# One background side for the adaLN blocks, unforced norm chains and one side for both attentions' heads in a two-layer hybrid DiT kernel

## The chip, the cores and the metric

The kernel runs on one core of a Trainium2 chip. The metric is the device time of one execution in microseconds: the median of the runs shown, and the profiled execution where the trace is read. TensorE (PE) multiplies, VectorE (DVE), ScalarE (ACT) and GpSimd (POOL) do the elementwise work, and SyncE (SP) issues nearly all of the transfers.

## The reference, cut to what matters

Two layers work on 256 latent tokens `x` and 256 context tokens `h`, each of 1024 channels, all in float32. In the last layer the context leaves after the mixer's inputs, so that what follows runs on 256 tokens instead of 512.

```python
for l in range(DEPTH):                                   # DEPTH = 2
    sh1, sc1, g1, sh2, sc2, g2, sh3, sc3, g3 = split(silu(c) @ w_mod[l] + b_mod[l], 9)   # and the same of c_ctx
    x = x + 0.5 * g1 * swiglu(modulate(rms_norm(x, norm_g[l, 0]), sh1, sc1), ...)        # and h
    y, yc = token_mixer(modulate(rms_norm(x, norm_g[l, 1]), sh2, sc2), ...)              # GLA, neighbourhood attention, GQA
    x = x + g2 * y                                       # h only if l < DEPTH - 1
    x = x + 0.5 * g3 * swiglu(modulate(rms_norm(x, norm_g[l, 2]), sh3, sc3), ...)
```

`token_mixer` projects `u` by `w_in`, runs the three branches (four GLA heads, 16 neighbourhood heads, eight GQA heads on two key heads), and merges them as a sum of `sigmoid(gate_i) * (y_i @ w_branch[i])`, times `w_out`. `w_mod[l]` is 1024 x 9216: 18 blocks of 512 columns a layer.

## The kernel before

**Weights.** Every large product is a chain of `chunk` items: a tile of 512 KB of weights (`w_raw`) is loaded through SP's queue, ScalarE rounds it to `w_hi`, GpSimd computes the rest `w_lo`, and TensorE multiplies three times (hi x hi, hi x lo, lo x hi). `RAW_BUFS` raw tiles and `SPLIT_BUFS` = 3 split pairs are in flight; a tile is loaded when the splitter has done with the one `RAW_BUFS` before it. The products are `up` and `dn` in the FFNs, `pf` (channels on partitions) and `pt` (tokens on partitions) elsewhere.

**Sides.** The order of instructions is fixed when the program is built. `Clock` keeps an estimated time for each engine, from `took`; its PE time is "now". Work beside the main chain is written as generators whose operations (`Gated`) yield until the clock says that their inputs are ready; VectorE, ScalarE and GpSimd operations of a side also yield while their engine's estimate is more than `QUEUE` = 1 us ahead. `tick`, called after every six products, resumes each of them once (`round`): first the `urgent` list, then the named `sides`. `finish(name)` gives a side the hurry and resumes it until it is over; where nothing can go on, the clock's PE time jumps (`round_or_stall`), and the engine stands idle on the chip. `flush` does this for the urgent list, and every `call` item begins with a `flush`.

**adaLN blocks.** `first_load` and `first_u` compute four blocks at the start. A block in `mod_gen` loads eight `mod_w` tiles (256 KB each) and sums them, scaled by `silu(c)` and `silu(c_ctx)`, into `mod_acc`: 16 VectorE operations on 128x512. After two blocks, TensorE reduces over partitions (`mod`), ScalarE copies, and TensorE transposes (`mod_t`). The steps are paced, `MOD_SPAN / len(extra)` us a block: twelve blocks in layer 0's first FFN, four in its last, ten in layer 1's first. `prog.finish(("ffn", l, i))` stands before the second half's `down`. Six blocks are held back as fillers: `mod_prefetch` loads their weights, and `norm_fill` multiplies them on TensorE inside a norm.

**Norms.** At the end of an FFN or of the mixer, `norm_start` puts two chains (`norm_chain`, tokens 0 to 255 and 256 to 511) on the urgent list: sums of squares on TensorE into `n_ss`, `rsqrt` on VectorE (`rs_v`, `rs_s`, `rs_y`, `rs_a`), a diagonal `n_diag`, its broadcast by TensorE, then `n_t`, `u_hi` and `u_lo` for each of eight channel tiles. The first chain stops after four tiles until the second has four. The next product calls `need(r, k)` for each tile.

**Mixer.** GLA heads run as side `gla` (two lanes) beside `gla_project` and `nat_project(l, 0)`; then side `nat` (eight pairs of heads, two lanes), and, after `finish("nat")` and `split_y1` in `ready1`, side `gqa` (eight heads, two lanes), which `ready2` finishes. In layer 0 `ready1` stands in branch 1 after two gates; in layer 1 it is `middle` of branch 0.

Of the kernel before, what the change touches and what calls it, by code (L numbers as in the profile page):

```python
# [18 lines left out]
P = 128  # L19
# [18 lines left out]

RAW_BUFS = 4
SPLIT_BUFS = 3  # L40
# [5 lines left out]
QUEUE = 1.0  # L46
MOD_SPAN = 270.0

# [5 lines left out]
class Clock:  # L54
# [59 lines left out]
    def took(self, engine, name, ins, outs):  # L114
        n = max([x.free_size() for x in ins + outs] + [1])
        if engine == "PE":
            return 0.11 if name == "transpose" else self.matmul(ins, outs[0])
        if engine == "ACT":
            return 0.18 + n / 1200 + (0.2 if len(outs) > 1 else 0.0)
        if engine == "POOL":  # L120
            return 0.1 + n * 0.00235
        both = sum(not x.space == bass.MemoryType.PSUM and x.free_size() > 64 for x in ins) > 1
        return 0.1 + n / 960 * (1.5 if both else 1.1)

# [76 lines left out]
class Program:  # L201
# [4 lines left out]
    def __init__(self, nc, rpool, wpool):  # L206
        self.nc = nc
        self.rpool = rpool
        self.wpool = wpool
        self.clock = Clock()  # L210
        self.items = []
        self.sides = {}
        self.urgent = []
        self.free = [0.0] * 4
        self.force = False
        self.first = False
        self.hurry = None
        self.wakes = []
        self.paced = {}
        self.kept = set()  # L220
        self.chains = {}
# [105 lines left out]
    def round(self):  # L327
        self.wakes = []
        n = self.clock.count
        self.first = True  # L330
        for g in list(self.urgent):
            if not self._resume(g):
                self.urgent.remove(g)
        self.first = False
        for name in list(self.sides):
            if name in self.sides:
                self._step(name)
        return self.clock.count > n

    def round_or_stall(self):  # L340
        sides, urgent = len(self.sides), len(self.urgent)
        if self.round() or len(self.sides) < sides or len(self.urgent) < urgent:
            return
        wakes = [w for w in self.wakes if w is not None]
        assert wakes, "the sides wait for each other"
        self.clock.t["PE"] = max(self.clock.now + 0.01, min(wakes))
# [83 lines left out]
def tile_backbone(ctx: ExitStack, tc: tile.TileContext, I: dict, out: bass.AP):  # L430
# [114 lines left out]

    st = {}

    def first_load():
# [15 lines left out]
        for j in range(4):  # L564

            ws = []
            for kt in range(KT):
                w = S("mod_w")
                src = I["w_mod"][0, kt * P : (kt + 1) * P, : 2 * D].rearrange("p (s n) -> p s n", s=2)
                sync.dma_start(w.rearrange("p (s n) -> p s n", s=2), src[:, :, j * 256 : (j + 1) * 256])  # L570
                ws.append(w)
            st["first_w"].append(ws)
            prog.load(2 * (j + 1) if j < 2 else 4)

# [121 lines left out]

    def mod_load(l, g):
        ws = []
        for kt in range(KT):
            w = S("mod_w")  # L700
            sync.dma_start(w, I["w_mod"][l, kt * P : (kt + 1) * P, g * 512 : (g + 1) * 512])
            ws.append(w)
        return ws

    def mod_gen(blocks, key, us):

        acc = []
        for l, g in blocks:
            yield from prog.pace(key, 0.0)
            ws = mod_load(l, g)  # L710
            acc += [S("mod_acc") for _ in range(2)]
            for kt in range(KT):
                yield from prog.pace(key, us / KT)
                for r in range(2):
                    c = scv[:, kt, r : r + 1]
                    a = acc[r - 2]
                    if kt == 0:
                        yield from gdve.tensor_scalar(a, ws[kt], c, None, op0=ALU.mult)
                    else:
                        yield from gdve.scalar_tensor_tensor(a, ws[kt], c, a, op0=ALU.mult, op1=ALU.add)  # L720
# [11 lines left out]
        for j, (l, g) in enumerate(blocks):  # L732
            bias = st["vec", l][:, 4 * g : 4 * g + 4].unsqueeze(2).broadcast_to([P, 4, 2])
            yield from gdve.tensor_tensor(st["mod", l][:, 4 * g : 4 * g + 4, :], src[:, :, j, :, 0], bias, op=ALU.add)
        prog.release(1)

    def mod_side(name, blocks, us):
        prog.side(name, lambda: (mod_gen(blocks[i : i + 2], name, us) for i in range(0, len(blocks), 2)))

# [71 lines left out]
    def norm_start(l, i, r, n):  # L811
        prog.later(norm_chain(l, i, r, n))

# [61 lines left out]

    def ffn(l, i, which, n, square, extra=(), ahead=(), lead=None):

# [126 lines left out]

        if extra and not lead:
            mod_side(("ffn", l, i), extra, MOD_SPAN / len(extra))
        for a, b in ((0, 12), (12, NH)):
            for mp in range(a // 2, b // 2):
# [5 lines left out]
                if both and lead:  # L1014
                    prog.call(lambda: load_vectors(1))
                    mod_side(("ffn", l, i), extra, MOD_SPAN / len(extra))
            if a == 0:
                prog.call(gates)
                if late_vectors:
                    prog.call(late_vectors.pop())  # L1020
            for fp in range(4):
                if a and fp == 0:
                    if extra:
                        prog.finish(("ffn", l, i))
                    mod_prefetch(("ahead", l, i), ahead)
# [599 lines left out]

    def nat_project(l, g, nq):

# [4 lines left out]

        for kind, c0, tiles in (("q", C_NQ, nq // P), ("k", C_NK, TT), ("v", C_NV, TT)):
            raw = []

# [142 lines left out]

    def gqa_head(h, need_ctx):
        kv = h // 4  # L1780
        res = [{}]
        yield from prog.until(lambda: ("qrot", h // 4) in st and ("qk", kv) in st)
        yield from turn_split("qq", h, st["qrot", h // 4], h % 4, None, False)
# [22 lines left out]

    def branch(l, i, n, ready=None, middle=None):

        th = {}

        def gate(mp):
            def ev(m, ps):
                t = S("m_t")[:, :n]
                act.activation(t, ps, AF.Tanh, scale=0.5)
                th[2 * mp + m] = t

            proj_f(l, C_GATE + D * i + 256 * mp, n, ev)

        def product(mp):
            def ev(m, ps):  # L1820
                f = 2 * mp + m
                t = th.pop(f)
                if i == 0:
# [20 lines left out]

        gate(0)
        gate(1)
        if ready:
            ready()
        product(0)
        product(1)  # L1850
        if middle:
            middle()
        for mp in (2, 3):
            gate(mp)
            product(mp)

    def merge_out(l, n):
# [13 lines left out]
        def last_fn(kh):  # L1871
# [18 lines left out]
            return fn  # L1890

        prog.call(gates)
        for mp in range(4):
            if mp == 3 and n > LAT:
# [16 lines left out]
    def mixer(l, ahead):  # L1911
# [4 lines left out]
        def reset():  # L1916
            st["y2"] = [None] * KT
            st["zs"] = {}
            st["gq"], st["gk"], st["gv"] = {}, {}, {}
            for key in [k for k in st if k == "fg" or k[0] in ("gw2", "nraw", "nv", "qrot", "qk", "qv")]:  # L1920
                del st[key]
# [5 lines left out]
        gla_project(l, 1, nq)  # L1927
        nat_project(l, 0, nq)
        prog.finish("gla")
        prog.finish(("nat", "q", 0))  # L1930
        prog.finish(("nat", "k", 0))
        prog.side("nat", lambda: (nat_pair(l, j, need_ctx) for j in range(8)), lanes=LANES)
        nat_project(l, 1, nq)

        def ready1():
            prog.finish("nat")
            prog.call(lambda: split_y1(n))
            for kind, first in (("k", 0), ("q", 0), ("q", 4)):
                prog.finish(("gqa", kind, first))
            prog.side("gqa", lambda: (gqa_head(h, need_ctx) for h in range(8)), lanes=LANES)  # L1940

        if need_ctx:
            gla_gate(l, nq)
            branch(l, 0, n)
            gqa_project(l, nq)
            branch(l, 1, n, ready=ready1)
        else:
            gqa_project(l, nq)
            gla_gate(l, nq)
            branch(l, 0, n, middle=ready1)  # L1950
            branch(l, 1, n)

        def ready2():
            prog.finish("gqa")

# [22 lines left out]
    prog.call(first_tokens)  # L1978
    blocks = iter([(l, g) for l in range(DEPTH) for g in range(18)])

    def take(n):
        return [next(blocks) for _ in range(n)]

    take(4)
    late_vectors = [lambda: turn_vectors(1)]
    for l in range(DEPTH):
        last = l == DEPTH - 1
        n = LAT if last else NT
        extra = take((12, 10)[l])
        ahead = take(1)  # L1990
        ffn(l, 0, 0, NT, (l, 1), extra, ahead, None if l else lead)
        norm(l, 1, NT, ahead)
        ahead = take(2 if last else 1)
        mixer(l, ahead)
        norm(l, 2, n, ahead)
        if last:
            ffn(l, 2, 1, n, None)
        else:
            extra = take(4)
            ahead = take(1)  # L2000
            ffn(l, 2, 1, n, (l + 1, 0), extra, ahead)
            norm(l + 1, 0, n, ahead)
    prog.run()
# [41 lines left out]
```

## Time and profile before

| | |
|---|---|
| median of three runs | 2944.79 us (2941.56 to 2947.43) |
| profiled execution | 2946.19 us |
| its span, first to last instruction | 2944.1 us |
| TensorE busy | 2773.4 us (94%), 15547 products |
| VectorE, GpSimd, ScalarE busy | 1644.7, 1287.3, 1008.3 us |
| mean granted clock of TensorE | 0.973 |
| bytes read from HBM | 342.83 MB |

The profiled execution takes 2.1 us more than its span. Busy TensorE is not TensorE at its peak: a product's record is longer than the distance to the next one, and at a granted clock of 0.5 it runs at 1.2 GHz instead of 2.4.

### The profile page before, as it was taken

Reading aid. Unit: us, or ns where it says so; the run is one execution under the profiler, and the core shown is the slowest. Engines: PE = TensorE matmul, PEld = TensorE weight load, DVE = VectorE, ACT = ScalarE, POOL = GpSimd, SP = SyncE. Lnnn points to the kernel's source line nnn. Section 1 sums busy time; section 2 is a strip of 40 time slices with the busy share of each in tenths; the row PEclk is TensorE's granted clock in tenths of the full one; section 3 lists DMA queues with packets and bytes.
Section 4 is the critical chain, followed back from the end, with each engine's and each line's share of the span. In section 5 each row is a group of like instructions: output and inputs, shape, how many; then the busy total and the mean of one; then the engine's idle time right before and its main releaser. Section 6 shows DMA issues by size and latency. Waiting matters only on the chain.

```text
span 2944.1 us, 39725 instructions
## 1 busy us (share of the span) xinstructions
PE 2773.4 (94%) x15547; PEld 2320.4 (79%) x15547; DVE 1644.7 (56%) x2969; ACT 1008.3 (34%) x1599; POOL 1287.3 (44%) x585
## 2 busy tenths in 40 slices
PE   8999768999999999998999979998899998899999
PEld 6888647777777788887878878886787777799899
DVE  5666646545785285446344266756455669764422
ACT  2222212343443244322223212222244345454443
POOL 3444313233333442333444434443333445548787
PEclk9999979999999999999999989999899999999999
DMA  7544532122222331333334325444322323336554
GB/s 240 173 151 151 185 108 73 53 65 81 75 71 71 89 89 58 97 97 108 126 118 129 115 87 169 167 155 148 100 72 79 91 78 114 93 113 208 177 182 151
DMA packets 295647, 346.46 MB, mean 118 GB/s; under 512 B 15541, under 2 KB 238806, under 8 KB 295460
## 3 DMA queue, kind: packets, MB, share of 16 engines
q1 hardware_dynamic: 294964, 343.58, 37.2%
q8 instruction: 122, 2.00, 0.3%
q14 instruction: 65, 0.53, 0.1%
q0 software_dynamic: 320, 0.28, 0.0%
q10 hardware_dynamic: 176, 0.07, 0.0%
HBM read 342.83 MB, written 1.05 MB: 117 GB/s over the span
## 4 chain that ended last, share of the span: by engine, by line
PE 85%; DVE 9%; issue 4%; POOL 1%; ACT 1%; DMA 0%; SPq 0%; DVEq 0%; POOLq 0%; ACTq 0%
PE up L169 27%; PE pf L169 19%; PE dn L169 14%; PE pt L169 14%; PE a_s L196 2%; DVE mod_acc L196 2%; PE a_t L196 2%; PE n_o L196 1%; PE g_o L196 1%; PE q_o L196 1%; DVE a_p L196 1%; POOL w_lo L196 1%; DVE rs_a L196 1%; PE g_U L196 1%; PE a_qk L196 1%
## 5 line engine op out<-in xcount | busy, mean ns | idle before, releaser
L196 POOL TENSOR_TENSOR w_lo<-w_raw,w_hi 128x1024 fp32r<-128x1024 f32 (+1 forms) x508 | 1227.5, 2421 | 1586.1 <-ACT w_hi L196 1496.4
L196 ACT CAST w_hi<-w_raw 128x1024 fp32r<-128x1024 f32 (+1 forms) x504 | 521.0, 1037 | 973.0 <-issue 327.6
L169 PE MATMUL up<-u_hi,w_lo 128*128 128x512 f32 (+1 forms) x1504 | 530.0, 352 | 10.1 <-POOL w_lo L196 10.1
L169 PE MATMUL up<-u_hi,w_hi 128*128 128x512 f32 (+1 forms) x1504 | 532.5, 354 | 2.7 <-DVE u_hi L169 2.5
L169 PE MATMUL up<-u_lo,w_hi 128*128 128x512 f32 (+1 forms) x1504 | 529.6, 352 | 0.9 <-DVE u_lo L196 0.7
L169 PE MATMUL dn<-ff_h,w_hi 128*128 128x512 f32 (+1 forms) x1528 | 400.4, 351 | 0.0
L196 DVE SCALAR_TENSOR_TENSOR mod_acc<-mod_w,scv,mod_acc 128x512 f32<-128x512 f32 x364 | 372.5, 1087 | 2.0 <-DMA mod_w<-w_mod 1.8
L169 PEld LDWEIGHTS up<-u_hi,w_hi 128*128 128x128 f32 x1504 | 286.6, 191 | 54.9 <-issue 15.3
L169 PEld LDWEIGHTS up<-u_hi,w_lo 128*128 128x128 f32 x1504 | 286.6, 191 | 48.9 <-POOL w_lo L196 11.2
L169 PEld LDWEIGHTS up<-u_lo,w_hi 128*128 128x128 f32 x1504 | 286.8, 191 | 38.2 <-DVE u_lo L196 0.9
L169 PEld LDWEIGHTS dn<-ff_h,w_hi 128*128 128x128 f32 x1528 | 269.7, 191 | 39.5 <-issue 1.7
L169 PE MATMUL dn<-ff_h,w_lo 128*128 128x512 f32 (+1 forms) x764 | 267.2, 350 | 0.0
L169 PE MATMUL pt<-w_hi,u_hi 128*128 128x512 f32 x640 | 261.5, 409 | 0.3 <-ACT g_q L169 0.3
L169 PE MATMUL pf<-u_hi,w_hi 128*128 128x256 f32 (+1 forms) x736 | 248.3, 337 | 4.1 <-DVE fg L169 1.8
L169 PE MATMUL pt<-w_hi,u_lo 128*128 128x512 f32 x640 | 250.1, 391 | 0.0
L169 PE MATMUL pt<-w_lo,u_hi 128*128 128x512 f32 x640 | 249.9, 391 | 0.0
L169 PE MATMUL pf<-u_hi,w_lo 128*128 128x256 f32 (+1 forms) x736 | 238.6, 324 | 5.6 <-POOL w_lo L196 5.6
L169 PE MATMUL pf<-u_lo,w_hi 128*128 128x256 f32 (+1 forms) x736 | 238.0, 323 | 0.0
L169 DVE TENSOR_TENSOR ff_h<-ff_a,up 128x512 f32<-128x512 f32 (+1 forms) x88 | 53.5, 621 | 323.2 <-PE up L169 287.6
L169 PE MATMUL pf<-y,w_hi 128*128 128x512 f32 (+1 forms) x768 | 194.3, 343 | 1.4 <-ACT y L196 1.2
L169 DVE SCALAR_TENSOR_TENSOR x<-dn,ff_g,x 128x256 f32<-128x256 f32 x112 | 47.1, 478 | 215.2 <-PE dn L169 215.2
L169 PEld LDWEIGHTS pf<-u_hi,w_hi 128*128 128x128 f32 x736 | 142.5, 194 | 23.7 <-issue 10.2
(226 smaller groups left out, 4017.1 us busy)
## 6 DMA issues: line engine op xcount, KB each, us to landing
w_raw<-ffn_w_in SPq DMA_DIRECT2D x176, 512.0 KB
w_raw<-w_in SPq DMA_DIRECT2D x168, 512.0 KB
mod_w<-w_mod SPq DMA_DIRECT2D x288, 256.0 KB
w_raw<-ffn_w_out SPq DMA_DIRECT2D x80, 512.0 KB
w_raw<-w_branch SPq DMA_DIRECT2D x48, 512.0 KB
w_raw<-w_out SPq DMA_DIRECT2D x16, 512.0 KB
w_raw<-ffn_w_out SPq DMA_DIRECT2D x16, 256.0 KB
n_rel<-nat_rpb SPq DMA_DIRECT2D x32, 109.5 KB
```

Of the source, the lines that this page charges most:

```text
L169: return real(*args, **kw)
L196: return real(*args, **kw)
```

## The change

`RAW_BUFS` goes from 4 to 3. VectorE's estimate in `took` goes up. `norm_start` appends to a list of its own, `norms`, which `round` resumes first and which `flush` does not drain. One side `mods` takes 26 blocks in order through the whole program, 42 us a block, resumed last in every round; it loads `mod_w` tiles three steps ahead instead of eight at once; it starts no new pair while `paused` (from `finish("gla")` to `ready2`). `mod_need` gives it the hurry where a norm, a gate or a residual needs its columns. The six fillers stay the same blocks. In the mixer the second group's neighbourhood `q` is projected before `finish("gla")`; the eight pairs and the eight GQA heads are one side, `heads`, with two lanes; `ready1` waits for all `y1` only. In layer 0 the GQA heads wait for the split `y1`; in layer 1 they don't, branch 0 has no stop, and branch 1 begins with all gates of branches 1 and 2.

```diff
-RAW_BUFS = 4
+RAW_BUFS = 3
...
-MOD_SPAN = 270.0
+MOD_PACE = 42.0
...
-        return 0.1 + n / 960 * (1.5 if both else 1.1)
+        return 0.15 + n / 960 * (1.8 if both else 1.15)
...
     def round(self):
...
-        for g in list(self.urgent):
-            if not self._resume(g):
-                self.urgent.remove(g)
+        for waiting in (self.norms, self.urgent):
+            for g in list(waiting):
+                if not self._resume(g):
+                    waiting.remove(g)
         self.first = False
-        for name in list(self.sides):
+        for name in sorted(self.sides, key=lambda name: name == "mods"):
...
-            prog.load(2 * (j + 1) if j < 2 else 4)
+            prog.load(min(2 * (j + 1), RAW_BUFS))
...
     def mod_gen(blocks, key, us):
         acc = []
+        yield from prog.until(lambda: key not in prog.paused or prog.hurry == key)
         for l, g in blocks:
             yield from prog.pace(key, 0.0)
-            ws = mod_load(l, g)
+            yield from prog.until(lambda: ("vec", l) in st)
+            ws = []
             acc += [S("mod_acc") for _ in range(2)]
             for kt in range(KT):
                 yield from prog.pace(key, us / KT)
+                while len(ws) < min(KT, kt + 3):
+                    k = len(ws)
+                    w = S("mod_w")
+                    sync.dma_start(w, I["w_mod"][l, k * P : (k + 1) * P, g * 512 : (g + 1) * 512])
+                    ws.append(w)
...
+    def mod_need(l, k0, k1):
+        def run():
+            prog.hurry = "mods"
+            while any((l, g) in st["mod_blocks"] and (l, g) not in st["mod_done"] for g in range(k0 // 4, k1 // 4)):
+                prog.round_or_stall()
+            prog.hurry = None
+        prog.call(run)
...
     def norm_start(l, i, r, n):
-        prog.later(norm_chain(l, i, r, n))
+        prog.norms.append(norm_chain(l, i, r, n))
...
             if a == 0:
+                mod_need(l, 24 * i + 16, 24 * i + 24)
                 prog.call(gates)
...
                 if a and fp == 0:
-                    if extra:
-                        prog.finish(("ffn", l, i))
+                    if square:
+                        mod_need(square[0], 24 * square[1], 24 * square[1] + 16)
...
-        gate(0)
-        gate(1)
+        done = st["gated"]
+        for b in gates or (i,):
+            for mp in range(4 if gates else 2):
+                if (l, b, mp) not in done:
+                    gate(mp, b)
+                    done.add((l, b, mp))
         if ready:
             ready()
...
         nat_project(l, 0, nq)
+        nat_project(l, 1, nq, "q")
         prog.finish("gla")
-        prog.finish(("nat", "q", 0))
-        prog.finish(("nat", "k", 0))
-        prog.side("nat", lambda: (nat_pair(l, j, need_ctx) for j in range(8)), lanes=LANES)
-        nat_project(l, 1, nq)
+        prog.call(lambda: prog.paused.add("mods"))
+        heads = [lambda j=j: nat_pair(l, j, need_ctx) for j in range(8)]
+        heads += [lambda h=h: gqa_head(h, need_ctx, (lambda: "y1" in st) if need_ctx else None) for h in range(8)]
+        prog.side("heads", lambda: (make() for make in heads), lanes=LANES)
+        nat_project(l, 1, nq, "kv")
...
         else:
             gqa_project(l, nq)
             gla_gate(l, nq)
-            branch(l, 0, n, middle=ready1)
-            branch(l, 1, n)
+            branch(l, 0, n)
+        branch(l, 1, n, ready=ready1, gates=None if need_ctx else (1, 2))

         def ready2():
-            prog.finish("gqa")
+            prog.finish("heads")
+            prog.call(lambda: prog.paused.discard("mods"))
```

## Rows read from the trace of the kernel before

**Rows 1.** The profile's page, part 1: busy time and its share, by engine.

```profile
PE 2773.4 (94%) x15547; PEld 2320.4 (79%) x15547; DVE 1644.7 (56%) x2969; ACT 1008.3 (34%) x1599; POOL 1287.3 (44%) x585
```

**Rows 2.** Waits of TensorE, whole span: total us, times, longest.

```profile
PE mod L196 <- DVE mod_acc L196: 55.8, 8, 20.6
PE n_ss L196 <- DVE n_diag L196: 37.4, 5, 8.8
...
PE up L169 <- POOL w_lo L196: 10.1, 4, 5.7
```

**Rows 3.** Timeline, layer 0's first FFN: start, us, instruction, idle before.

```profile
338.53 4.02 SPq L169 DMA_DIRECT2D mod_w<-w_mod  x8
...
338.64 1.07 PE L196 MATMUL mod<-mod_acc,ones 128*32 128x512 f32 x8 [1.25 <-DVE mod_acc L196]
...
342.18 0.88 DVE L196 TENSOR_SCALAR mod_acc<-mod_w,scv 128x512 f32<-128x512 f32 x2 [0.17 <-DMA mod_w<-w_mod]
...
373.74 1.94 PE L196 MATMUL mod<-mod_acc,ones 128*32 128x512 f32 x8 [19.74 <-DVE mod_acc L196]
...
398.10 1.94 PE L196 MATMUL mod<-mod_acc,ones 128*32 128x512 f32 x8 [20.55 <-DVE mod_acc L196]
...
401.49 1.20 PE L169 MATMUL dn<-ff_h,w_hi 128*128 128x512 f32 x2
```

**Rows 4.** Timeline of TensorE at the same place of layer 1.

```profile
2057.41 1.94 PE L196 MATMUL mod<-mod_acc,ones 128*32 128x512 f32 x8 [9.58 <-DVE mod_acc L196]
...
2060.82 1.20 PE L169 MATMUL dn<-ff_h,w_hi 128*128 128x512 f32 x2
```

**Rows 5.** Tile `mod_acc` up to 420: ns min/median/max, first and last start.

```profile
L196 DVE SCALAR_TENSOR_TENSOR mod_acc<-mod_w,scv,mod_acc x168: 735/741/2911, 73.1 to 397.2; 128x512 f32<-128x512 f32 x168
...
L196 PE MATMUL mod<-mod_acc,ones x48: 592/617/1062, 134.9 to 399.0; 128*32 128x512 f32 x48
```

**Rows 6.** Chain that ended last, two pieces: start, us, products.

```profile
239.16 21.55 PE up L169 x95
...
401.84 18.23 PE dn L169 x72
```

**Rows 7.** Timeline, norm before layer 0's mixer.

```profile
469.20 0.15 DVE L196 TENSOR_SCALAR rs_v<-n_ss 128x2 f32<-128x2 f32 x1
...
472.68 1.22 PE L196 MATMUL n_ss<-n_diag,ones 128*128 128x256 f32 x2 [8.77 <-DVE n_diag L196]
...
473.83 3.64 PE L169 MATMUL mod<-mod_w,scv 128*32 128x512 f32 x16
```

**Rows 8.** Windows: busy PE, PEld, DVE, ACT, POOL; clock; DMA share; GB/s.

```profile
455.00:478.00 23.00, 12.59 (x81) 8.65 (x81) 18.77 (x59) 3.07 (x5) 5.72 (x4) 0.70 0.20 55
...
540.00:600.00 60.00, 56.28 (x412) 45.22 (x411) 38.50 (x91) 22.12 (x37) 12.66 (x6) 1.00 0.16 45
...
2440.00:2540.00 100.00, 86.56 (x581) 74.40 (x580) 93.69 (x197) 48.43 (x88) 59.12 (x27) 0.91 0.39 115
2540.00:2560.00 20.00, 14.02 (x94) 10.62 (x94) 10.73 (x31) 8.62 (x19) 8.15 (x7) 0.83 0.31 89
...
2760.00:2940.00 180.00, 179.64 (x1495) 179.04 (x1494) 48.53 (x59) 77.62 (x106) 146.83 (x63) 1.00 0.55 172
```

**Rows 9.** Tiles `g_oT`, `n_raw`, `q_o` in layer 0: first and last start.

```profile
L196 PE MATMUL g_oT<-ident,g_o x32: 270/272/330, 585.5 to 691.7; 128*128 128x128 f32 x32
...
L169 DVE COPY n_raw<-pt x2: 692/692/692, 701.6 to 704.3; 128x512 f32<-128x512 f32 x2
...
L196 PE MATMUL q_o<-a_pt,q_v x72: 277/283/285, 1168.1 to 1207.7; 128*128 128x256 f32 x72
```

**Rows 10.** Costliest groups of the page: busy, mean ns, idle before.

```profile
L196 POOL TENSOR_TENSOR w_lo<-w_raw,w_hi 128x1024 fp32r<-128x1024 f32 (+1 forms) x508 | 1227.5, 2421 | 1586.1 <-ACT w_hi L196 1496.4
L196 ACT CAST w_hi<-w_raw 128x1024 fp32r<-128x1024 f32 (+1 forms) x504 | 521.0, 1037 | 973.0 <-issue 327.6
...
L196 DVE SCALAR_TENSOR_TENSOR mod_acc<-mod_w,scv,mod_acc 128x512 f32<-128x512 f32 x364 | 372.5, 1087 | 2.0 <-DMA mod_w<-w_mod 1.8
```

## What the change should do, worked out before it ran

> **What bounds the kernel now.** I read the page first: TensorE is busy 94% of the span, so only its holes can be won [rows 1]. I then took the table of waits for TensorE, because it says which engine ends each hole [rows 2]: VectorE's modulation sums (`mod_acc`) 55.8 us, the norm's `n_diag` 37.4 us in five waits, POOL's `w_lo` 10.1 us. The timeline and the windows put places to them.
>
> The largest hole is in the first FFN. At its second `down`, `prog.finish` asks for all twelve modulation blocks, and two of the six pairs aren't summed yet: TensorE sits idle 19.74 us, does the pair's small products, sits 20.55 us more, and its first `dn` product starts at 401.49 [rows 3]. With the idle time that began at 373.74 - 19.74 = 354.0 that is 47.5 us. The same happens in layer 1's first FFN: 9.58 us, back at work at 2060.82, so 13.0 us from 2047.83 [rows 4]. Why pairs come late is seen in the sums: they begin at 73.1, the first pair's products stand at 134.9, the fourth's at 338.64 [rows 3, 5], so a pair takes (338.64 - 134.9)/3 = 67.9 us, where `MOD_SPAN` asks for 45. A product of 512 columns takes 21.55/95 = 0.227 us [rows 6], the sides are looked at every six of them, 1.36 us, and a step due after 2.81 us is taken at the third look, 4.08; sixteen are 65.3.
>
> Four norms each have a hole: after the second half's sums of squares TensorE waits 8.77 us for `n_diag`, then comes the block held for filling (473.83 to 477.47), and only then the first `pf` product [rows 7]. `flush` writes the whole chain out before anything else. In layer 1's attention TensorE is busy 86.56 of 100 us and then 14.02 of 20, at clocks 0.91 and 0.83, while VectorE is busy 93.69 of 100 [rows 8].
>
> **The change, part by part.** The sum is made against the profiled execution, 2946.2 us (span 2944.1 and 2.1 around it), which is 1.4 over the median of the runs.
>
> Side over the whole program, 42 us a block: a step is due after 5.25 us and taken at the fourth look, 5.44; a pair is 16 x 5.44 = 87 and the 2.6 that it took beyond its steps before. The first pair's last step is the fifteenth after its start, so the pairs stand near 73 + 82 = 155, 245 and 334. The gates of the first half want blocks 4 and 5 (about 170), the second `down` wants 6 to 9, three pairs, at 354: in time by some 20 us. The hole of 47.5 us then goes. Its two pairs' products stay (1.07 us for `mod` at the full clock [rows 3], about half of that for `mod_t`, 3.0 in all); the 72 `dn` products behind the hole took 18.23 instead of 16.3 us [rows 6], which comes back too: **-46.5 us**. Layer 1's sums now start in layer 0, pause for the attentions and go on when its GQA heads end, at 1207.7 before [rows 9] and some 60 us sooner now; the six pairs that are left take 6 x 89.6 = 538 us and stand near 1690, long before the second `down` at 2047. The 13.0 us less 1.5 for the pair's products, and some 1.5 of slow clock back as behind the first hole: **-13 us**. The fillers are the same six blocks as before, and cost the same.
>
> Where this work goes: 26 blocks of some 16 x 1.09 = 17 us of VectorE [rows 10], of which some four pairs pass into layer 0's norms, its GLA part and its third FFN. VectorE was busy 38.50 of 60 us in the GLA part [rows 8]; eleven steps of two sums, 11 x 2 x 1.087 = 24 us, fill it to 62.5. The sums come last in every round, so they slide rather than the heads, but the heads slow too. The cover: GLA's last product stood at 691.7, the projection that hides it ended at 704.3 [rows 9], 13 us later, and the moved `q` projection adds 4 x 24 x 0.227 = 22 us before `finish("gla")`. Of the 35 us I let the heads use up nearly all and charge **+5** (bounds 0 and 24, the sums' whole share of that stretch). These sums' median is 741 ns and their longest 2911 [rows 5], next to POOL's `w_lo` of 2421 on average [rows 10]: a sum can stand a whole `w_lo` long. The Trainium skill ("SBUF — State Buffer", "Who interferes with whom") calls this an exclusive lock between VectorE with two inputs in SBUF and GpSimd, the second one blocked to the end. By it every sum put into the GLA part could hold a head's operation for 2.4 us; by the rows' mean of 1.087 it is 0.35 over the median. I go by the mean.
>
> Norm chains not forced: the fill (3.64 us) and the first half's four `k` steps (4 x 12 x 0.120 = 5.8 us, 0.120 from 180 us over 1495 products [rows 8]) can now run in the hole: 9.4 us for 8.77. But the second half's `rs_v` starts at 469.20 only; its broadcast ends at 472.68 + 1.22 = 473.9, and three short VectorE steps on, near 476, stands its first `u` [rows 7]: TensorE waits again for some 3 us. That leaves some 6 a norm where no sums run beside it (the last of the four). In the other three, four steps of sums (8 to 9 us of VectorE) fall into the chain, and I leave them 3. 6 + 3 x 3.3 = **-16 us**, bounds 0 and 4 x 8.77 = -35. Behind the norm the mixer's short loads on SP, POOL's memsets for the decay weights and ScalarE's table load now pass the rest of the chain; the chain waits for none of them, so I put nothing on them.
>
> Shared side and gates first: layer 0's attentions have no hole to win, and their order hardly changes (GQA heads still wait for `y1`). In layer 1 the stop in the middle of branch 0 goes, and two gates (four loads of weights) more stand before `finish("heads")`. To be won are 13.4 + 6.0 us of idle time, and the clock, 100 x 0.09 + 20 x 0.17 = 12 us at most, part of it in idle time [rows 8]: 28 together. VectorE at 94% is not relieved, so I take less than half: **-12 us**, bounds 0 and -28.
>
> VectorE's new price (0.15 + 1.8 n/960: 1.11 us for a sum of 512) fits the mean of 1.087 [rows 10]; the old one was 0.9. The other five waits for `mod_acc`, 55.8 - 49.9 = 5.9 us [rows 2 to 4], should mostly go: -4. Loading `mod_w` three at a time instead of eight (eight took 4.02 us of the queue of SP [rows 3]) lets `w_raw` pass: `w_lo`'s 10.1 us shrink by -4 [rows 2]. **-8 us**, bounds 0 and -12.
>
> Three raw buffers instead of four: tightest where a load of weights is used up in 24 x 0.120 = 2.9 us, in the last FFN. A buffer's round is a cast (1.04), a `w_lo` (2.42) [rows 10] and the transfer. The first of eight loads issued at 338.53 was there at 342.18 [rows 3], 3.65 us, behind a large one. 1.04 + 2.42 + 3.65 = 7.1 is under 3 x 2.9 = 8.6: **0**; if the round were 1 us over, its 60 loads would cost 0.33 each, 20 us. At the start, the fourth load isn't needed before a buffer of the split is free.
>
> Sum: -46.5 - 13 + 5 - 16 - 12 - 8 = -90.5. 2946.2 - 90.5 = 2855.7, and 1.4 off for the median: **2854 us**.
>
> **The rivals.**
> - Only the two stops go (A). The norm's hole moves behind its first four steps and layer 1 stays bound by VectorE, which speaks for it at 94% busy; TensorE's idle time while VectorE is free in the norms speaks against. -46.5 - 13 - 8 + 5 = -62.5: 2882.
> - All holes go (B): -46.5 - 13 - 35 - 28 - 8 = -130.5: 2814. The clock would have to stay full.
> - The pairs aren't in time (C), so that the side does not do what it says at 354: one pair is awaited at full speed, as the second of the old hole was (401.49 - 377 = 24 us). 2854 + 24 = 2878. A look more per step, 6.8 us, would do it; a margin of one pair's quarter speaks for it, the rate of before, which the count of looks explains to 4%, against.
> - Slower than before (D): dearer VectorE prices make the planner hold the heads back, and in layer 1 they end with nothing but four products of branch 1 (23 us) to hide them. Its heads took some 310 us, from about 2330 to 2640 (the last hole of [rows 8] ends at 2560, eight GQA heads later comes `ready2`). A 512-column sum's price rises by 1.11/0.9 = 1.23, a two-column step's from 0.10 to 0.15, 1.5. If the heads stretched by 1.3, they would be 93 us late at `finish("heads")`: 2854 + 12 + 93 = 2959. It decides from (2945 - 2866)/310 = 1.25 on. Against it: the prices only come near what the operations take, and those of one input rise by about 1.1.
> - A gap left in a norm costs more than itself (E). Around a norm the granted clock is 0.70 over 23 us, and it was 0.83 in 20 us of layer 1 with holes in them [rows 8]; what was lost there is 20 x 0.17 = 3.4 us. If each norm's 3 us gap cost 3.4 more, 2854 + 4 x 3.4 = 2868. The Trainium skill ("TensorE: Matmul & The Clock Gate", Part 1) has an idle TensorE fall to 1.2 GHz and come back only after sustained work, and the `dn` products after the long hole [rows 6] agree.
>
> **How the numbers follow.** Forecast 0.52, A 0.20, B 0.12, C 0.07, D 0.04, E 0.05. The likeliest by itself spans 2836 to 2872 (norms and layer 1 each half wrong). For 8 in 10 I go up to past A and C, with most of GLA's 24 on top of the lower one (2882 + 14), and down to B: 2814 to 2896. Measured runs differ by 0.2%, about 6 us, which is what can't be told from no change. Faster 0.94 (all cases but D, and 0.02 of A and C, where the GLA part would add its worst), same 0.02, slower 0.04.
>
> **What would show it.** Right: no wait for `mod_acc` over 3 us near 350 and 1950; TensorE's waits for `n_diag` well under 37 us, with `pf` or `up` products between a norm's sums of squares and its second broadcast; sums of `mod_acc` all through the GLA part and the third FFN; VectorE near 55 of 60 us there; last FFN as long as before. Wrong: a wait before `a_qk` or at the last `g_oT` of layer 0; idle time after the last gate of layer 1 while `a_t` and `q_o` finish; `w_hi` waiting for `w_raw`.

## The result, and the profile after

The changed kernel takes 2882.24 us (median of four runs, 2878.06 to 2883.48), against 2946.11 for the kernel before beside it: a ratio of 0.9783 [0.9766, 0.98], so 63.9 us less. The forecast was 2854, with 2814 to 2896 as the range. Two thirds of the forecast gain came; the missing third has one place, which the parts of the span show. They are cut at the same product of each kernel's trace (a norm runs from the start of the last main product ahead of it to the end of the next 192 main products, 96 in the last):

```
us of the profiled execution           before   after   forecast change   measured
layer 0, first FFN                      434.0   378.4        -50.5          -55.6
layer 1, first FFN                      361.5   346.5        -13            -15.0
the five norms                          205.3   213.3        -20             +8.0
layer 0, mixer and its output           817.2   819.2         +5             +2.0
layer 1, mixer and its output           568.9   560.6        -12             -8.3
start, other FFNs                       551.9   553.0          0             +1.1
```

(The forecast's -8 for prices and loads is split here as it was made: -4 for the sums' other waits to the first FFN, -4 for `w_lo` to the norms.) Every line but one is within 6 us. The norms were to give 20 and took 8. The profiled execution is the fastest of the four, so its parts add up to 67.8 us and not to 63.9.

TensorE's waits over the whole span say what stands there now (total us, times, longest). They are to be read against [rows 2]:

```profile
PE up L169 <- POOL w_lo L196: 16.0, 4, 6.8
PE pf L169 <- POOL w_lo L196: 8.7, 3, 4.8
...
PE pf L169 <- DVE u_hi L196: 7.0, 3, 4.6
PE pf L169 <- DVE u_lo L196: 5.7, 6, 2.4
...
PE n_ss L196 <- DVE n_diag L196: 5.1, 3, 4.2
PE up L169 <- DVE u_lo L196: 4.8, 5, 2.4
...
PE up L169 <- DVE u_hi L196: 4.1, 5, 1.2
...
PE mod L196 <- DVE mod_acc L196: 2.7, 2, 2.1
```

`mod_acc` has gone from 55.8 us to 2.7 and `n_diag` from 37.4 to 5.1, as the prediction asked. But `w_lo` has gone from 15.7 us to 24.7, and the `u` tiles of the norms from 0.9 to 21.6, so these two took up 29.7 of the 32.3 us that `n_diag` gave. (The 15.7 are the 10.1 in `up` of [rows 2] and, in the kernel before, these in `pf`.)

```profile
PE pf L169 <- POOL w_lo L196: 5.6, 4, 2.0
```

The side itself is in time. This is the tile `mod_acc` (first and last start), and then the first `dn` of the second half in TensorE's timeline, 53.6 us sooner than in [rows 3] and with no idle time before it:

```profile
L196 PE MATMUL mod<-mod_acc,ones x104: 592/605/617, 145.6 to 1814.5; 128*32 128x512 f32 x104
```

```profile
347.69 0.39 PE L169 MATMUL up<-u_hi,w_lo 128*128 128x512 f32 x1
347.92 0.61 PE L169 MATMUL dn<-ff_h,w_hi 128*128 128x512 f32 x2
```

The first three pairs' products stand at 145.6, 234.5 and 323.2, where 155, 245 and 334 were forecast. The last pair stands at 1814.5 and not near 1690, and is still 190 us ahead of the second `down` of layer 1 (2004.71).

These windows answer to [rows 8] (us; busy time of PE, of PEld, which loads its weights, of DVE, ACT and POOL; granted clock, DMA share, GB/s). Four lie in the GLA part, one in layer 0's last FFN, two in layer 1's attention, and the last in layer 1's last FFN.

```profile
480.00:540.00 60.00, 56.90 (x425) 49.03 (x425) 44.77 (x89) 23.00 (x39) 14.74 (x6) 0.97 0.27 84
540.00:600.00 60.00, 60.00 (x338) 47.48 (x338) 36.97 (x72) 29.05 (x47) 19.34 (x8) 1.00 0.28 84
600.00:660.00 60.00, 59.95 (x318) 45.65 (x319) 45.16 (x113) 21.24 (x32) 17.44 (x7) 1.00 0.29 83
660.00:720.00 60.00, 60.00 (x283) 48.80 (x282) 52.08 (x92) 22.38 (x36) 29.70 (x14) 1.00 0.45 132
1360.00:1420.00 60.00, 60.00 (x267) 49.69 (x266) 36.57 (x37) 16.93 (x22) 27.66 (x11) 1.00 0.44 145
2380.00:2480.00 100.00, 90.30 (x642) 78.84 (x642) 94.23 (x195) 52.14 (x97) 58.06 (x26) 0.92 0.39 116
2480.00:2500.00 20.00, 20.00 (x164) 17.98 (x163) 10.37 (x29) 9.31 (x15) 13.13 (x9) 1.00 0.53 147
2691.00:2871.00 180.00, 179.93 (x1501) 179.72 (x1500) 50.44 (x61) 77.81 (x106) 147.45 (x63) 1.00 0.56 175
```

The GLA part stays TensorE's (from 540 on busy 60 of 60 at full clock), and the sums slide there: the two pairs summed beside it take 149 and 164 us instead of 89. In layer 1, VectorE is as full as before for 100 us, with TensorE busy 90.30 of them instead of 86.56, and the hole behind them (14.02 of 20, clock 0.83) is gone.

**One norm, read closely.** The norm between layer 0's mixer and its last FFN grew most, 42.8 to 50.3 us. Its timeline, first half:

```profile
1272.75 5.02 POOL L196 TENSOR_TENSOR w_lo<-w_raw,w_hi 128x1024 fp32r<-128x1024 f32 x2 [11.48 <-ACT w_hi L196]
...
1273.19 2.31 DVE L196 TENSOR_TENSOR rs_a<-rs_a,rs_v 128x2 f32<-128x2 f32 x1
...
1275.53 2.26 DVE L196 SCALAR_TENSOR_TENSOR rs_y<-rs_a,rs_y 128x2 f32<-128x2 f32 x1
...
1278.37 1.22 PE L196 MATMUL n_ss<-n_diag,ones 128*128 128x256 f32 x2 [4.22 <-DVE n_diag L196]
```

Two VectorE steps on two columns, 0.16 us otherwise, take 2.3 us each while GpSimd computes `w_lo`. Sums ran before them (two at 1271.86), so that they slid into the two `w_lo`. This is the second half, with the two `w_lo` apart (from narrower windows):

```profile
1299.06 2.00 ACT L196 CAST w_hi<-w_raw 128x1024 fp32r<-128x1024 f32 x2 [24.18 <-PE up L169]
...
1300.19 7.29 POOL L196 TENSOR_TENSOR w_lo<-w_raw,w_hi 128x1024 fp32r<-128x1024 f32 x1 [22.41 <-ACT w_hi L196]
...
1301.76 0.88 DVE L196 TENSOR_SCALAR mod_acc<-mod_w,scv 128x512 f32<-128x512 f32 x2
1302.55 2.74 DVE L196 SCALAR_TENSOR_TENSOR mod_acc<-mod_w,scv,mod_acc 128x512 f32<-128x512 f32 x4
...
1307.44 2.37 POOL L196 TENSOR_TENSOR w_lo<-w_raw,w_hi 128x1024 fp32r<-128x1024 f32 x1
...
1307.54 0.58 PE L169 MATMUL up<-u_hi,w_lo 128*128 128x256 f32 x1 [6.76 <-POOL w_lo L196]
```

ScalarE's rounding of the next two weights waits 24.18 us for TensorE's `up`. The first two weights serve both halves of the tokens (channel tiles 0 to 3), the third stands ready beside them, and the fourth, without which tiles 4 to 7 can't be multiplied, gets a split pair only when the second half is done with the first. Its `w_lo` then falls into the row of `u_hi`, `u_lo` and sums on VectorE and takes 7.29 us. It ends 2.2 us after the last sum (1302.55 + 2.74 = 1305.29), which is about its usual time, and the next one, with nothing beside it, takes 2.37. In the kernel before the same two ran after that row:

```profile
1349.92 4.71 POOL L196 TENSOR_TENSOR w_lo<-w_raw,w_hi 128x1024 fp32r<-128x1024 f32 x2 [21.50 <-ACT w_hi L196]
```

So TensorE waits 6.76 us and starts again at the lower level of its clock: products of 256 columns follow each other at 0.21 us instead of 0.12 until 1313.46, at a granted clock of 0.50.

### The profile page after: what moved, and what is told of

It reads as the page before. It is cut to its first block, busy times and chain, and to the rows that moved or that the text cites. A ratio compares the mean times of both kernels' runs of the same rounds, so it can differ in the third digit from the quotient of the medians.

```text
span 2876.3 us, 39661 instructions
## 1 busy us (share of the span) xinstructions
PE 2777.6 (97%) x15547; PEld 2330.8 (81%) x15547; DVE 1662.6 (58%) x2970; ACT 1007.2 (35%) x1598; POOL 1288.1 (45%) x585
## 4 chain that ended last, share of the span: by engine, by line
PE 86%; DVE 8%; issue 4%; POOL 1%; DMA 0%; ACT 0%; SPq 0%; DVEq 0%; POOLq 0%; ACTq 0%
PE up L169 28%; PE pf L169 17%; PE dn L169 15%; PE pt L169 15%; PE a_s L196 2%; PE a_t L196 2%; PE n_o L196 1%; POOL w_lo L196 1%; PE g_o L196 1%; PE q_o L196 1%; PE g_U L196 1%; PE a_qk L196 1%; DVE rs_a L196 1%; DVE z L169 1%; DVE a_p L196 1%
```

## The experiments

All were timed beside the kernel before; medians and ratios to it.

**Norm chains forced again** (2890.95 us, 0.9811 [0.9797, 0.9825]).

```diff
-        prog.norms.append(norm_chain(l, i, r, n))
+        prog.later(norm_chain(l, i, r, n))
```

> The changed kernel with the norm chains back on the urgent list, so that each call item drains them; all else as changed (2882 us). Seen so far, by stages of the two traces (from the last product before a norm to the end of the next 192 products): norms 42.6, 42.8, 49.6, 46.2 us before and 46.6, 50.3, 47.0, 43.7 after, where the prediction took 16 us off them. Theory 1 (VectorE's background sums slip between the steps of the norm chain): forcing the chain does not keep the sums out, so the three norms with sums stay at 47 to 50 or get longer, and the fourth goes back to 46: 2882 to 2895. Theory 2 (an unforced chain computes its u tiles while GpSimd makes w_lo of the next weights, and the two engines block each other): the three norms go back to about 43: 2865 to 2872. Theory 3 (three raw buffers): no change, 2882.

8.7 us slower than the changed kernel. The unforced chain is a gain, if a small one, so it isn't what lengthened the norms. With forced chains they take 219.5 us, and in two of them TensorE waits for a pair of sums (11.50 and 11.86 us for `mod_acc`).

**No sums while a norm chain is open** (2862.31 us, 0.9715 [0.9701, 0.9729]): one line in `mod_gen`, behind the step's `pace`.

```diff
+                yield from prog.until(lambda: not prog.norms or prog.hurry == key)
```

> The changed kernel, with the background sums held back as long as a norm chain is unfinished (one more wait in mod_gen before each step); same work. Theory 1: the norms of layer 0 and the first of layer 1 fall from 46.6, 50.3 and 47.0 us to 40 or less each, as the fourth one without sums gained 2.5 to 4: 2860 to 2868. Theory 2: the sums matter little, w_lo in the norms still takes about 4.8 us a piece instead of 2.4, and TensorE waits 5 to 7 us for it as now: 2878 to 2884. Theory 3: 2882.

19.9 us less than the changed kernel: that is what the sums in the norms cost, where the prediction charged some 3 us in each of three. Of the 15.1 us between the two profiled executions, 11.2 lie in the norms and 3.8 in layer 1's first FFN. The norms fall to 202.1, only 3 less than before. The waits say what remains:

```profile
PE up L169 <- POOL w_lo L196: 14.9, 4, 6.0
PE pf L169 <- DVE u_lo L196: 8.3, 8, 2.3
PE pf L169 <- POOL w_lo L196: 8.0, 2, 6.0
```

`w_lo` has hardly moved (22.9 us, after 24.7), and the edit doesn't reach all of it. In the norm read above the chain now ends without sums, but four of them follow it at once, and the late `w_lo` still waits for their end:

```profile
1292.03 6.49 POOL L196 TENSOR_TENSOR w_lo<-w_raw,w_hi 128x1024 fp32r<-128x1024 f32 x1 [19.50 <-ACT w_hi L196]
...
1293.58 2.74 DVE L196 SCALAR_TENSOR_TENSOR mod_acc<-mod_w,scv,mod_acc 128x512 f32<-128x512 f32 x4
```

What the edit does take away are the sums' delays in the chain itself: the waits for `n_diag` fall from 5.1 us to 0.9, and those for `u_hi` from 11.1 to 6.8.

**Four raw buffers** (2881.62 us, 0.9778 [0.9765, 0.9792]).

```diff
-RAW_BUFS = 3
+RAW_BUFS = 4
```

> The changed kernel with four raw weight buffers instead of three. Theory 3 (with three buffers the split of the third and fourth load behind a norm comes later): TensorE's waits for w_lo, 24.7 us in seven waits now, fall back towards the 16 us of before, and the time to 2868 to 2874. Theories 1 and 2, and the prediction, which put nothing on this part: 2882 within 4.

No difference: the term of 0 holds, and the waits for `w_lo` (24.7 us here too) are not a matter of raw tiles.

**The kernel before with the list of norms alone** (2946.08 us, 0.9997 [0.9988, 1.0006]).

```diff
...
-        prog.later(norm_chain(l, i, r, n))
+        prog.norms.append(norm_chain(l, i, r, n))
```

> The kernel before (2946) with one part of the change alone: norm chains on a list of their own that call items don't drain. No background sums run in its norms (all are finished before), except for those that start right behind the norm before layer 1's first FFN. Prediction: 6 us off each of the four norms, 2922. Theory 1 (only the sums spoil it): 3 to 6 us off each, 2922 to 2934. Theory 2 (the u tiles collide with w_lo): between 2 us longer and 2 us shorter each, 2938 to 2954, with w_lo in the norms at 4 to 5 us a piece.

No gain, for two reasons. The waits show the first:

```profile
PE mod L196 <- DVE mod_acc L196: 62.3, 9, 20.6
PE up L169 <- POOL w_lo L196: 17.0, 6, 7.1
...
PE n_ss L196 <- DVE n_diag L196: 10.9, 5, 3.6
PE pf L169 <- POOL w_lo L196: 9.2, 6, 4.8
```

`n_diag` loses 26.5 of its 37.4 us, and `w_lo` takes 10.5 of them (15.7 to 26.2) and the `u` tiles 7.8 (0.9 to 8.7). The norms gain 10.6 (205.3 to 194.7). The second reason is the stop in layer 1's first FFN, which takes 8.8 back (361.5 to 370.3): TensorE waits 13.18 us there for the last pair instead of the 9.58 of [rows 4], and its `dn` begins at 2060.26 instead of 2060.82. Why the sums, which begin with the FFN, were no sooner wasn't tried.

**The side alone** (2893.65 us, 0.9818 [0.9805, 0.9832]): the kernel before with `mods`, `mod_need` and the pause, all else as before.

> The kernel before with the background side over the whole program alone: norm chains still forced, the two attentions apart as before, four raw buffers, the old VectorE prices. Theory 1 (the parts add up: the side removes both stops, and pays for it in the norm chains, where its sums stand): stops -71 as in the changed kernel, norms +12 as in the run with forced chains, layer 0's mixer +1 to +7, layer 1's unchanged, so 2946 - 71 + 12 + 4 = 2891, between 2887 and 2896. Theory 2 (the shared heads and the early gates are only affordable, or only gain, with the rest; layer 1's gain of 9 comes of the sums being over before it): layer 1's mixer gets its 9 us here too and the kernel takes 2880 to 2884. Theory 3 (the old prices pack the sums so that a pair comes late): a wait for the sums stays at one of the stops, 2900 or more.

The sum is as the first theory had it: both stops in the FFNs are gone (434.0 to 378.7, 361.5 to 341.4), the norms take 7.9 more and layer 0's mixer 8.9. One long wait for `mod_acc` is left, 11.99 us at 418.33, in the norm behind the first FFN.

**The old mixer's order** (2896.72 us, 0.983 [0.9812, 0.9848]) and **the old VectorE prices** (2890.46 us, 0.9809 [0.9793, 0.9825]) in the changed kernel.

```diff
-        heads = [lambda j=j: nat_pair(l, j, need_ctx) for j in range(8)]
...
+        prog.side("nat", lambda: (nat_pair(l, j, need_ctx) for j in range(8)), lanes=LANES)
...
+            branch(l, 0, n, middle=ready1)
```

> The changed kernel with the attentions' order of before (two sides, the early query projection and the gates first undone); the sums still pause from the end of the GLA part to the end of the GQA heads. Theory 1 (the shared heads are worth what layer 1's mixer gained, 9 to 10 us, and cost layer 0 nothing): 2891 to 2893, layer 1's mixer back at 545, layer 0's as in the changed kernel. Theory 2 (layer 1 gained because no sums ran there and VectorE's prices are new): 2880 to 2884, and the order of the heads is worth nothing. Theory 3 (the shared side cost layer 0 something that hid its gain): layer 0's mixer under 770 and layer 1's at 545, about 2886.

```diff
-        return 0.15 + n / 960 * (1.8 if both else 1.15)
+        return 0.1 + n / 960 * (1.5 if both else 1.1)
```

> The changed kernel with the VectorE prices of before. Theory 1 (the new prices set the order a little better but carry no part): within 3 us of the changed kernel, 2879 to 2885. Theory 2 (they carry layer 1's gain, since they hold the sums and heads off TensorE's queue until they are done): layer 1's mixer 540 or more, 2888 to 2893. Theory 3 (dearer prices hold the heads back, as the rival of the prediction had it): the old ones are faster, 2870 to 2876.

The order is worth 9.5 us in layer 1 and 6.7 in layer 0; the prices 13.0 in layer 0's mixer (819.2 against 832.2), none in layer 1. Undone one at a time, the chain's freedom, the order and the prices cost 8.7, 14.5 and 8.2; all three undone, in the side alone, cost only 11.4. They don't add, and which of them gives what isn't settled.

**A fourth split pair** in the version without sums in the norms (2838.25 us, 0.9632 [0.9619, 0.9646]).

```diff
-SPLIT_BUFS = 3
+SPLIT_BUFS = 4
...
-SLOTS = 54
+SLOTS = 52
```

> The version without sums in the norm chains (2862.3 us), with a fourth pair of buffers for split weights, paid for with two of the 54 slots. In that version TensorE waits 6.2 us in each of three norms for the w_lo of the fourth weights: its cast starts only when the first norm half's products have given a split buffer back, and the two w_lo then take 4.4 us each instead of 2.35. Theory 1 (the hole that n_diag left has passed to the split buffers): the three waits of 6.2 us and their slow clock go, 2838 to 2848. Theory 2 (behind w_lo stands VectorE's u, so that TensorE waits as long for that): 2858 to 2863, with waits for u_lo in place of w_lo. Theory 3 (two slots fewer hold the heads back): the norms gain, the mixers lose, 2862 or more.

It takes another 24.1 us off and is the fastest kernel of all. The norms take 168.6, 33.5 less; layer 0's mixer gives 9.0 of that back and its first FFN 4.7, and whether the two slots given up cost them that was not tried. This is the same norm as above, its first half and the broadcast of the second:

```profile
1272.55 2.36 POOL L196 TENSOR_TENSOR w_lo<-w_raw,w_hi 128x1024 fp32r<-128x1024 f32 x1 [11.48 <-ACT w_hi L196]
...
1272.97 2.08 DVE L196 TENSOR_SCALAR u_hi<-n_t,mod 128x256 fp32r<-128x256 f32 x1
...
1276.13 2.38 POOL L196 TENSOR_TENSOR w_lo<-w_raw,w_hi 128x1024 fp32r<-128x1024 f32 x1 [1.22 <-ACT w_hi L196]
...
1283.84 0.70 PE L196 MATMUL n_ss<-n_diag,ones 128*128 128x256 f32 x2 [0.27 <-DVE n_diag L196]
```

The fourth weights are split at 1276.13, early in the first half, and in the whole span no wait for `w_lo` is left. The clock follows, as the window over this norm shows in the changed kernel and then in this one:

```profile
1270.50:1320.80 50.30, 36.44 (x231) 32.77 (x231) 32.75 (x88) 7.45 (x10) 14.65 (x4) 0.76 0.21 69
```

```profile
1270.20:1305.50 35.30, 30.91 (x231) 27.77 (x230) 26.49 (x71) 7.40 (x10) 13.68 (x4) 0.95 0.17 50
```

The same 231 products in 15.0 us less, at a clock of 0.95 for 0.76. The Trainium skill ("TensorE: Matmul & The Clock Gate", Part 1) has the clock come back only after sustained work, and the two windows agree: a hole inside a norm is paid for again by the products behind it.

**Four split pairs with the sums left in** (2845.03 us, 0.9649 [0.9636, 0.9662]): the changed kernel with the two numbers above.

> The changed kernel (2882.2 us) with a fourth pair of buffers for split weights and two slots fewer; the sums run in the norm chains as in the changed kernel. The same edit took 24 us off the version without sums in the norms. Theory 1 (two separate losses, buffers and sums): 2882 - 24 = 2858, between 2853 and 2862. Theory 2 (the sums hurt only through the late split, since they lengthen w_lo): with the split done early they cost little, 2838 to 2848. Theory 3 (the sums delay the norm's own VectorE steps, and the waits just change their name to n_diag and u): 2866 or more.

37.2 us below the changed kernel, and only 6.8 above the version without sums there. The total is the second theory's, but its reason is not shown. In the norms the sums cost 17.3 us here (185.9 against 168.6), more than the 11.2 with three pairs, and `n_diag` is waited for 8.2 us instead of 2.1. The totals come so close because layer 0's mixer is 10.6 us shorter here than in the version without sums; the reason for that was not looked for.

**Four split pairs in the kernel before** (2924.42 us, 0.9919 [0.9905, 0.9932]), with three raw buffers.

> The kernel before with four pairs of buffers for split weights, three raw buffers and 52 slots, all else as it was. Theory 1 (the fourth pair matters only where an unforced chain lets TensorE come to the fourth weights before the second half is ready): 2940 to 2950, no change. Theory 2 (it is worth its gain by itself, forced chain or not): four norms by 6 each, 2918 to 2926.

The first theory falls: 24.3 us less with the chains still forced. The norms take 18.7 of it (205.3 to 186.6). The fourth weights were late there too, and the waits say so:

```profile
PE n_ss L196 <- DVE n_diag L196: 31.0, 5, 6.6
...
PE pf L169 <- POOL w_lo L196: 0.2, 1, 0.2
```

`w_lo` goes from 15.7 us to 0.2, with one raw tile fewer, and `n_diag` from 37.4 to 31.0. So the waits for `w_lo` in [rows 2] came of the split pairs and not of late loads.

**Forced chains in the fastest version** (2853.84 us, 0.9681 [0.9667, 0.9694]): a count of open chains holds the sums, and the chains go on the urgent list.

```diff
...
-        prog.norms.append(norm_chain(l, i, r, n))
+        def chain():
+            yield from norm_chain(l, i, r, n)
+            prog.chained -= 1
+
+        prog.chained += 1
+        prog.later(chain())
```

> The fastest version so far (2838.3 us: no sums in the norm chains, four split buffers) with its norm chains forced again, the sums still held while a chain runs. This prices the edit that the prediction put at -16. Theory 1 (with the buffers there, the unforced chain fills the hole at n_diag, 8.8 us in each of four norms, and the clock that it costs): 2869 to 2881. Theory 2 (the unforced chain is worth the 16 of the prediction even so): 2850 to 2858. Theory 3 (the gain was that of sums and buffers alone): 2836 to 2843.

15.6 us slower, with the hole of [rows 7] back:

```profile
1282.43 1.22 PE L196 MATMUL n_ss<-n_diag,ones 128*128 128x256 f32 x2 [8.49 <-DVE n_diag L196]
```

So the unforced chain is worth the -16 of the prediction, once the split is there and the sums are not. By parts it is 4.1, 3.8 and 3.8 us in the second to fourth norm. The first grows by 15.0 and the mixer behind it shrinks by 10.6, 4.4 for both; a longer wait for `mod_acc` (6.95 us, after 3.76) has a share in these.

**The kernel before with faster sums** (2926.58 us, 0.9925 [0.9912, 0.9939]).

```diff
-MOD_SPAN = 270.0
+MOD_SPAN = 170.0
```

> The kernel before with one number changed: the span over which each FFN spreads its sums, 170 us for 270. A step of the first FFN is then due after 1.77 us, taken at the second look, 2.72, and a pair takes some 46 us instead of 68. Theory 1 (the stops are a matter of pace, and a side per FFN could have been in time): six pairs end at 73 + 6 x 46 = 349, about when the second down comes; the stop of 47 us shrinks to under 5, that of 13 goes, and the kernel takes 2885 to 2900. Theory 2 (VectorE can't take two sums in 2.7 us beside the FFN's own work): a pair takes 60 us or more, the stop stays at 25 or more, and it takes 2915 to 2935.

The time is the second theory's, and the pace of a pair lies between the two: (373.5 - 115.2)/5 = 51.7 us. The last pair is still awaited:

```profile
373.46 1.94 PE L196 MATMUL mod<-mod_acc,ones 128*32 128x512 f32 x8 [17.21 <-DVE mod_acc L196]
...
376.86 1.20 PE L169 MATMUL dn<-ff_h,w_hi 128*128 128x512 f32 x2
```

The first FFN gains 24.8 of the 55.6. While it sums, VectorE is busy 239 of 303 us; in the changed kernel 155 of 275. This pace alone doesn't do it, and a faster one wasn't tried; taking blocks out of this FFN does. In layer 1 the last pair is no longer late (1983.7, the second `down` at 2039.8), but that FFN is only 1.4 us shorter, and why was not looked into.

## Why the prediction was partly right

- **The two stops, -46.5 and -13:** right in mechanism, and counting the steps (5.44 us each, 89.6 a pair) gave the first three pairs' times to 11 us. The last came 125 us later than forecast, since sums slid in the GLA part, and had the room for it. The first stop's gain was put 5.1 too low, with the -4 for other waits: I left two pairs' small products in this FFN (3.0) and did not count a third's (1.5), and all three now stand in the norm and the mixer behind it.
- **GLA and attention of layer 0, +5:** measured +2.0. The side alone adds 8.9 there. That the order and the prices take 7 to 13 of it back was not in the prediction, which held that layer 0's order hardly changes and put nothing on it; undoing it costs 6.7 there. I also forecast VectorE near 55 of 60; it was 37 to 52, since the sums slid.
- **Norms, -16: the step that failed.** Its first half, that fill and first-half products can run in the hole of `n_diag`, is right: that wait went from 37.4 to 5.1, and the edit is worth 15.6 by itself where nothing else is late. Two things were missed. I counted the steps whose activations were ready, and not the weights behind them: with three split pairs the fourth weights are split only when the second half is done with the first, in the middle of the row of `u` steps. A fourth pair (with two slots fewer) was worth 24 us in two versions and 37 in the third. And I priced the sums in the chain by their mean, as VectorE time; with three pairs they cost 19.9. The prediction weighed a row's mean of 1.087 us for a sum against the rule that a VectorE step and a `w_lo` block each other to the end, and went by the mean. In the norm the rows follow the rule: a step of 0.16 us takes 2.31, and a `w_lo` of 2.37 takes 7.29. The Trainium skill ("SBUF — State Buffer", "Who interferes with whom") has this lock, and the trace agrees. In the GLA part, where the prediction chose the mean, no loss of that size shows (+2.0 in layer 0's mixer, +8.9 in the side alone), but which of the two rules its heads follow wasn't measured.
- **Rival A (2882)** gave the number by luck, and half the cause: the norm's hole did move behind the first four steps, as it said. But layer 1's mixer did gain (8.3) and the norms lost as much (8.0), where A had nothing for either, and what stands in the norm is not only the second half's chain.
- **Shared heads, -12:** -8.3 in the table, 9.5 by undoing the order, and none of it from the prices. VectorE stayed full (94 of 100); TensorE won 3.7 us beside it and 6.0 in the hole behind it.
- **Prices and loads, -8:** the waits for `mod_acc` fell to 2.7 us as forecast; `w_lo`'s rose. The prediction put the 10.1 us of `w_lo` down to loads that block the queue of SP. The runs show the split pairs in their place: a fourth raw tile changed nothing, and a fourth split pair in the kernel before took `w_lo` from 15.7 to 0.2. The prices were worth 8.2, 13.0 in layer 0's mixer, where I had put nothing on them, less 4.7 in the norms.
- **Raw buffers, 0:** right. **Rivals C, D and E:** no pair was late, and no head was held back; E's extra clock is real, and part of what the fourth pair gave back.

## What to carry to other kernels

When a stall is to be filled with the next stage's work, follow every operand of that work to where it is made: here the activations were ready and the split weights weren't, and most of the hole changed its name from `n_diag` to `u` and `w_lo`. A gain ahead of a stop that another engine sets is taken back at the stop (10.6 won, 8.8 returned), so remove the stop first and then measure the rest. Background work that is cheap in the long products is dear in a short chain of tiny steps; hold it there.

## What the runs showed of the hardware

I had not expected a VectorE step on two columns to last 2.31 us, the length of the GpSimd operation beside it, nor a `w_lo` to take three times its 2.37 us (7.29) in a row of short VectorE steps. It wasn't held for one step but for the whole row, also by steps that started later than it did: in the three versions read it ended 2.19, 2.20 and 2.27 us after the row's last sum (the changed kernel, the one without sums in the chains, and that with a fourth pair). Nor is it only steps with two tensors: `u_hi`, with one, took 2.08 us for its usual 0.35 beside a `w_lo` of 2.36.
